# Counting table loads in the order, negating A's scores, four token tiles in the weights' room, and tile 5 of B's pairs 0 and 2 turned by VectorE and DMA

## The chip, the cores and the metric

The kernel runs on one core of one Trainium2 chip. The metric is the device time of one execution in microseconds (us). The core has five engines with a queue of instructions each: TensorE (PE in the profile), VectorE (DVE), ScalarE (ACT), GpSimd (POOL) and SyncE (SP), which here issues all DMAs.

## What is computed

One layer of a streaming encoder, for 1024 prompt tokens and 32 sample tokens with shared weights; the cache holds 512 earlier tokens for the sample. Everything is float32.

```python
u = rmsnorm(h, g_pre) @ w_in          # 1024 -> 4096: qA kA vA gA qB kB vB gB
# A: band attention, 8 heads x 64, chunks of 64, the own chunk and 8 before it
s = (qA @ kA.T) * SCALE + bias_table[:, clip(k_pos - q_pos, -128, 128) + 128]
oA = softmax(where(ok, s, -1e30)) @ vA
# B: stick-breaking attention, 8 heads x 64, strictly causal
z = (qB @ kB.T) * SCALE
log_1m = where(causal, log_sigmoid(-z), 0)
after = reversed_cumsum(log_1m) - log_1m
oB = where(causal, exp(log_sigmoid(z) + after), 0) @ vB
y = concat(oA * silu(gA), oB * silu(gB)) @ w_out
h = h + rmsnorm(y, g_post)
h = h + sigmoid(h @ w_ple_gate) * (p @ w_ple)
```

It returns the prompt's and the sample's h and the new keys and values of A and B.

## The kernel before

**Precision and layout.** Float32 products are made from two halves: a high part rounded to the type F32R (names with h) and the rest (names with l). The normalised input lies transposed in `hnh`/`hnl`, in three chunks of 352 tokens. A projection such as `kA1` (keys of A's pair 1) takes 24 matmuls of 352 columns per chunk into one of two `mm` banks (`col_steps`, L712), and ScalarE copies each bank into `stkA1`, `stqA1` or `stvA1`.

**Stages.** Heads go in pairs. The order of stages is A's pair 0, B's pair 0, A1, B1, A2, B2, A3, B3 (`pairs`, L1187). While the attention of one pair runs, the projections of the next pair are woven in (`weave`, L1255); behind the last pair come the gates, `w_ple`, the output product and the gate product of the last step.

**Attention of one head** (`attention`, L778). Its 1024 queries are eight tiles of 128. For tile i, `scores` (L813) makes the scores against the key blocks that it may see: all i+1 blocks in B, at most five in A. Scores of up to 512 columns lie in one of three banks `S` (names SA.., SB..), longer ones in two.
- In A, VectorE adds the bias and takes the row maximum in one instruction, a tiny TENSOR_SCALAR of one column negates it into `statA`, ScalarE makes Exp(score - maximum) with the row's sum, VectorE the reciprocal, GpSimd the product.
- In B, ScalarE makes Sigmoid(-z) into `om` and Sigmoid(z) into `be`, VectorE scans `om` backwards, and GpSimd multiplies. `om` and `be` are two arenas (`ring0`, 3,076 columns, and `ring1`, 3,640) from which each tile takes room in turn; room is free again when the tile that had it is done with.

**Turning the weights** (`weights_t`, L860). The value product needs the weights transposed, as `wTh` and `wTl`. There are two ways. The usual one is on TensorE: one transpose per block of 128 x 128, four to a bank `T` (names ptwA, ptwB), then ScalarE copies the bank to `wTh` and VectorE subtracts to get `wTl`. Tiles named in `ROUND` (L31) go round instead: VectorE transposes squares of 32 x 32 from `be` to `om` (STREAM_TRANSPOSE), one DMA writes that to DRAM (`swapB`), four DMAs read it back into `be` with the squares in place, and ScalarE's copy and VectorE's subtraction take it from there. Before, that was tile 5 in A and tiles 4 and 6 in B. `values` (L910) then makes the value product (PVA, PVB) for tiles 0 to 3 and for tiles 4 to 7.

**The order.** Nothing is issued where it is written. `Recorder` (L264) records every operation, with what it depends on and a class; `order` (L372) plays the whole program through with estimated durations (`cost`) and, whenever an engine is free, takes from what is ready the operation of the lowest class and earliest place. The result is the fixed order of each engine's queue; `emit` (L440) issues it, so all work has one line, L450, in the profile. After the change that line is L464. The estimates knew nothing of the instruction ACT_TABLE_LOAD, which stands in ScalarE's program wherever an Exp follows a Sigmoid or the reverse.

**Loading x.** `load_x` (L565) brings the nine token tiles in. Tiles 3 and 4 lie in the room that `wTh` will have later (`x34`, 33 x 128 columns); the others are in the `om` arena, which holds three tiles of 1,024 columns, so that tile 5 follows tile 0.

Of the kernel before, what the change touches and what calls it, by code (L numbers as in the profile page):

```python
# [13 lines left out]
P = 128  # L14
# [13 lines left out]

ROUND = {"A": ((5,),), "B": ((4,),(6,))}  # L31
LAG_T = 2
LAG_V = 2
SPACE_S = 0.1
# [138 lines left out]


class Op:
    __slots__ = ("eng", "what", "args", "kw", "key", "busy", "late", "ready", "left", "after", "at", "size", "shared")


LAND = {"PE": 165, "ACT": 0, "DVE": 0, "POOL": 0, "SP": 0, "CTL": 0}
SEM = 60  # L180
MARGIN = 400
ISSUE = 550
DMA_NS, DMA_RATE, DMA_MARGIN = 1500, 320.0, 2000
DVE_SET, POOL_SET = 137, 110

# [78 lines left out]
class Recorder:  # L264


    def __init__(self):
        self.ops, self.cls, self.low, self.closed, self.turns = [], 0, 0, [], []
        self.tensor = Engine(self, "PE", "tensor")
        self.vector = Engine(self, "DVE", "vector")  # L270
        self.scalar = Engine(self, "ACT", "scalar")
        self.gpsimd = Engine(self, "POOL", "gpsimd")
        self.sync = Engine(self, "SP", "sync")
# [26 lines left out]
    def node(self, eng, what, args, kw, after):  # L300
        o = Op()
        o.eng, o.what, o.args, o.kw, o.after = eng, what, args, kw, after
        o.key = (self.cls if eng == "PE" else self.low, len(self.ops))
        o.shared = False
        self.ops.append(o)
        return o

    def add(self, eng, what, args, kw):
        writes, reads = [], []
        method = what[1] if isinstance(what, tuple) else ""  # L310
        for i, a in enumerate(args):
            if isinstance(a, (View, Raw, Segments)):
                (writes if i == 0 or (method == "tensor_tensor_reduce" and i == 7) else reads).append(a)
        for k, a in kw.items():
            if isinstance(a, (View, Raw, Segments)):
                (writes if k in ("out", "accum_out") else reads).append(a)
        o = self.node(eng, what, args, kw, set())
        for mine, write in ((reads, False), (writes, True)):
            for v in mine:
                b = v.buf  # L320
                hit = False
                for other, box, wrote in b.uses:
                    if other is not o and (write or wrote) and all(p < y and x < q for (p, q), (x, y) in zip(v.box, box)):
                        o.after.add(other)
                        hit = True
                if b.pool is not None:
                    if not hit:
                        o.after.add(b.place)
                    b.pool.ops.append(o)
                b.uses.append((o, v.box, write))  # L330
        o.busy, o.late = self.cost(eng, method, args, kw, writes, reads)
        o.shared = eng == "POOL"
        if eng == "DVE":
            sbuf = [v for v in reads if isinstance(v, (View, Segments)) and not v.buf.psum and v.free() > 4]
            o.shared = len(sbuf) > 1 or (method == "tensor_copy" and len(sbuf) == 1 and not writes[0].buf.psum)
# [36 lines left out]
    def order(self):  # L372

        import heapq
        for place, old in self.turns:
            place.after.update(x[0] for x in old.uses)
        users = {id(o): [] for o in self.ops}
        for o in self.ops:
            o.left, o.ready = len(o.after), 0.0
            for a in o.after:  # L380
                users[id(a)].append(o)
        names = ("PE", "ACT", "DVE", "POOL", "SP", "CTL")
        free = dict.fromkeys(names, 0.0)
        soon = {e: [] for e in names}
        now = {e: [] for e in names}
        for o in self.ops:
            if not o.left:
                heapq.heappush(soon[o.eng], (0.0, o.key, id(o), o))
        out, port, line = [], 0.0, 0.0
        while len(out) < len(self.ops):  # L390
            best = None
            for e in names:
                if now[e]:
                    t = free[e]
                elif soon[e]:
                    t = max(free[e], soon[e][0][0])
                else:
                    continue
                if best is None or t < best[0]:
                    best = (t, e)  # L400
            t, e = best
            while soon[e] and soon[e][0][0] <= t:
                _, key, n, o = heapq.heappop(soon[e])
                heapq.heappush(now[e], (key, n, o))
            o = heapq.heappop(now[e])[2]
            if o.shared and e == "DVE" and port > t + DVE_SET:
                held = [x for x in now[e] if not x[2].shared]
                if held:
                    heapq.heappush(now[e], (o.key, id(o), o))
                    pick = min(held)  # L410
                    now[e].remove(pick)
                    heapq.heapify(now[e])
                    o = pick[2]
            o.at = t
            if e == "CTL":
                done = t
            elif e == "SP":
                free[e] = t + o.busy
                line = max(line, t + o.busy + DMA_NS) + o.late
                done = line + DMA_MARGIN  # L420
            else:
                if o.shared:
                    t = max(t, port - (DVE_SET if e == "DVE" else POOL_SET))
                    port = t + o.busy
                free[e] = t + o.busy
                done = t + o.busy + o.late
            out.append(o)
            for u in users[id(o)]:
                if u.eng == e and e != "SP":
                    r = t if e == "CTL" else free[e]  # L430
                else:
                    r = done + (0 if u.eng == "CTL" else SEM + (MARGIN if u.eng == "PE" else 0))
                u.ready = max(u.ready, r)
                u.left -= 1
                if not u.left:
                    heapq.heappush(soon[u.eng], (u.ready, u.key, id(u), u))
        return out
# [18 lines left out]
def stream_step(  # L456
# [108 lines left out]
    def load_x(t):  # L565
        n = min(P, T - t * P)
        if t == 3:
            x34.append(at.tile([P, ringh.cols], F32, tag="wTh", name="x34"))
        xt = x34[0][:, (t - 3) * D:(t - 2) * D] if 3 <= t < 5 else ring0.tile([P, D], f"x{t}")
        dma(xt[0:n], x_prompt[0, t * P:t * P + n, :] if t < 8 else x_sample[0])  # L570
        return xt, n

# [33 lines left out]
    def bias_rows():  # L606

        rb = ring0.tile([8, 257], "rb")
        dma(rb, rel_bias[0])
        R = ring1.tile([8, 768], "R")  # L610
        nc.gpsimd.memset(R, 0.0)
        nc.vector.tensor_scalar(R[:, 256:768], R[:, 256:768], rb[:, 0:1], None, ALU.add)
        nc.vector.tensor_copy(R[:, 0:256], rb[:, 0:256][:, ::-1])
        dma(r_dr, R)

# [96 lines left out]
    def col_steps(j):  # L712
# [7 lines left out]
        def mms(c, part):  # L720
# [24 lines left out]
                nc.gpsimd.tensor_tensor(sg, sg, box["og"], ALU.mult)  # L745
                dma(og_dr[n, :, cs], sg)
            elif k == "q":
                nc.scalar.activation(box["st"][:, cs], acc, AF.Copy, scale=SCALE)
            else:
                nc.scalar.copy(box["st"][:, cs], acc)  # L750

# [26 lines left out]
    def attention(ab, p, h):  # L778
# [5 lines left out]
        def begin():  # L784
            if ab == "A":
                bias = at2.tile([P, 640], F32, tag="bias", name=f"bias{nm}", bufs=2)
                dma(bias, bias_src(2 * p + h, P, 0, 640))
                nc.gpsimd.memset(bias[0:HD, 0:HD], NEG)
                nc.gpsimd.memset(bias[HD:P, 576:640], NEG)
                box["bias"] = bias  # L790

        def lo_block(i):
            return max(0, i - 4) if ab == "A" else 0

        together = {i: g for g in ROUND[ab] for i in g}
        whole, done_with = {}, []

        def cost(i):
# [14 lines left out]
        def scores(i):  # L813
# [27 lines left out]
            else:  # L841
                m = small.tile([P, 4], F32, tag="stat", name=f"stat{nm}_{i}", bufs=6)
                for j, (a, b, s) in enumerate(pieces):
                    nc.vector.tensor_tensor_reduce(
                        w0[:, a:b], s, box["bias"][:, n - b:n - a][:, ::-1], 1.0,
                        -3e38 if j == 0 else m[:, j - 1:j], ALU.add, ALU.max, m[:, j:j + 1])
                last = len(pieces) - 1
                nc.vector.tensor_scalar(m[:, 2:3], m[:, last:last + 1], -1.0, None, ALU.mult)
                nc.scalar.activation(w1[:, 0:n], w0[:, 0:n], AF.Exp, bias=m[:, 2:3], accum_out=m[:, 3:4])
                nc.vector.reciprocal(m[:, 3:4], m[:, 3:4])  # L850
                nc.gpsimd.tensor_scalar(w1[:, 0:n], w1[:, 0:n], m[:, 3:4], 1.0, ALU.mult, ALU.mult)
            state[i] = w0, w1
# [96 lines left out]
    def sample_attention(ab, gi):  # L949
# [45 lines left out]
        def scores():  # L995
# [20 lines left out]
            else:  # L1016
                m = small.tile([P, 4], F32, tag="stat", name="stat" + nm, bufs=6)
                for j, (a0, b0, s) in enumerate(pieces):
                    nc.vector.tensor_tensor_reduce(
                        w0[:, a0:b0], s, bx["bias"][:, NK - b0:NK - a0][:, ::-1], 1.0,  # L1020
                        -3e38 if j == 0 else m[:, 0:1], ALU.add, ALU.max, m[:, j:j + 1])
                nc.vector.tensor_scalar(m[:, 2:3], m[:, 1:2], -1.0, None, ALU.mult)
                nc.scalar.activation(w1[:, 0:NK], w0[:, 0:NK], AF.Exp, bias=m[:, 2:3], accum_out=m[:, 3:4])
                nc.vector.reciprocal(m[:, 3:4], m[:, 3:4])
                nc.gpsimd.tensor_scalar(w1[:, 0:NK], w1[:, 0:NK], m[:, 3:4], 1.0, ALU.mult, ALU.mult)
            bx["w1"] = w1
# [829 lines left out]
```

## Time and profile before

| what | us |
|---|---|
| median of 3 runs | 794.32 |
| lowest and highest run | 794.28, 794.92 |
| the profiled execution, whole | 794.5 |
| its span, first to last instruction | 792.7 |

The profile is of one execution. Its span leaves out 1.8 us around it. By stage (busy us of each engine; the stretches are cut near the first score matmul of each pair, the last near the output product; the start, and the stretch from 570 to 617 with the gates, are left out):

| stage | us | PE | DVE | ACT | POOL | DMA share |
|---|---|---|---|---|---|---|
| A0 | 60-109 | 48.22 | 37.08 | 36.23 | 35.41 | 0.88 |
| B0 | 109-173 | 62.70 | 52.90 | 47.67 | 43.12 | 0.64 |
| A1 | 173-229 | 56.00 | 43.32 | 40.87 | 39.39 | 0.77 |
| B1 | 229-308 | 78.16 | 62.70 | 57.58 | 58.51 | 0.71 |
| A2 | 308-353 | 43.47 | 33.28 | 37.91 | 24.32 | 0.61 |
| B2 | 353-420 | 66.51 | 50.49 | 49.12 | 32.28 | 0.41 |
| A3 | 420-478 | 56.41 | 44.51 | 41.72 | 24.41 | 0.53 |
| B3 | 478-570 | 91.86 | 67.52 | 56.25 | 55.34 | 0.60 |
| output and gate products | 617-793 | 170.67 | 137.59 | 112.85 | 106.54 | 0.69 |

How to read it: an engine's busy time is the sum of its instructions' stretches; matmuls overlap, so a busy PE says that something was under way, and what one matmul costs is read from start to start. In a row of the timeline stand the start in us, the duration, the engine, the line, the operation, what it writes <- what it reads, and in square brackets how long the engine was idle before it and for whom it waited. SPq stands for SyncE's queue, where the duration is that of issuing. Buffer numbers are left out of names, so that kA stands for every pair.

### The profile page before, as it was taken

The numbers are of one execution on the slowest core, as the hardware profiler recorded it, in microseconds if no ns is written. First come the engines' busy times: TensorE is split into PE (matmuls) and PEld (weight loads), VectorE is DVE, ScalarE is ACT, GpSimd is POOL, SyncE is SP. The second block draws the span as 40 slices with busy tenths as digits, with TensorE's granted clock in tenths as the row PEclk, the third lists the DMA queues.
The fourth block names the chain that finished last, engine by engine and source line by source line (L and its number), as shares of the span: only waits on it lengthen the run. The fifth ranks groups of instructions, "written<-read, shape, count | busy, mean of one in ns | idle before, by whom it ended". The sixth has DMA issues, their size and how long they took to land.

```text
span 792.7 us, 14512 instructions
## 1 busy us (share of the span) xinstructions
PE 778.6 (98%) x4606; PEld 717.9 (91%) x4606; DVE 587.4 (74%) x1170; ACT 537.3 (68%) x1173; POOL 470.1 (59%) x554
## 2 busy tenths in 40 slices
PE   8999999999999999999999999999999999999997
PEld 7999999899989998999998999999998787888786
DVE  7717778787778686877867788767565677988965
ACT  6636786786797677887766778664436976777551
POOL 5625867675777677454635246657462529599533
PEclk9999999999999999999999999999999999999999
DMA  8419866767866858544514746756589866859853
GB/s 296 138 49 289 215 188 213 189 189 226 229 192 205 232 176 238 144 128 123 142 54 132 172 111 175 225 167 188 151 261 291 282 190 186 288 168 336 272 170 133
DMA packets 161087, 153.66 MB, mean 194 GB/s; under 512 B 38562, under 2 KB 127178, under 8 KB 161011
## 3 DMA queue, kind: packets, MB, share of 16 engines
q1 hardware_dynamic: 161010, 152.73, 64.5%
q8 instruction: 37, 0.61, 0.3%
q14 instruction: 40, 0.32, 0.1%
HBM read 94.45 MB, written 49.83 MB: 182 GB/s over the span
## 4 chain that ended last, share of the span: by engine, by line
PE 84%; ACT 5%; DMA 3%; POOL 3%; DVE 3%; issue 2%; SPq 1%; DVEq 0%; ACTq 0%; POOLq 0%
PE mm_gA L450 6%; PE mm_gB L450 5%; PE mm_qB L450 5%; PE mm_vA L450 5%; PE mm_kB L450 5%; PE mm_qA L450 5%; PE PVB L450 4%; PE mm_kA L450 4%; PE SB L450 3%; PE mm_vB L450 3%; PE PVA L450 3%; PE SA L450 3%; PE g1P L450 2%; PE o3P L450 2%; PE o1P L450 2%; PE g0P L450 2%
## 5 line engine op out<-in xcount | busy, mean ns | idle before, releaser
L450 POOL TENSOR_TENSOR be<-be,om 128x1024 f32<-128x1024 f32 (+8 forms) x66 | 80.3, 1221 | 67.4 <-DVE om L450 34.0
L450 DVE TENSOR_TENSOR_SCAN om<-om,SB 128x384 f32<-128x384 f32 (+5 forms) x96 | 92.2, 966 | 14.5 <-ACT be L450 5.5
L450 POOL TENSOR_SCALAR be<-be,statA 128x640 f32<-128x640 f32 (+3 forms) x64 | 43.9, 691 | 52.8 <-DVE statA L450 37.0
L450 ACT ACTIVATE om<-SB 128x384 f32<-128x384 f32 (+5 forms) x96 | 46.6, 497 | 20.1 <-DVE SB L450 15.6
L450 ACT ACTIVATE be<-SB 128x384 f32<-128x384 f32 (+5 forms) x96 | 46.5, 498 | 13.4 <-DVE om L450 7.2
L450 ACT ACTIVATE be<-om,statA 128x640 f32<-128x640 f32 (+3 forms) x64 | 44.6, 697 | 15.5 <-DVE statA L450 11.3
L450 DVE TENSOR_TENSOR wTl<-ptwA,wTh 128x512 fp32r<-128x512 f32 (+2 forms) x80 | 36.2, 480 | 9.2 <-ACT wTh L450 8.9
L450 ACT CAST wTh<-ptwA 128x512 fp32r<-128x512 f32 (+2 forms) x80 | 32.1, 426 | 12.1 <-PE ptwA L450 10.4
L450 DVE TENSOR_TENSOR wTl<-ptwB,wTh 128x512 fp32r<-128x512 f32 (+3 forms) x64 | 33.7, 546 | 4.7 <-ACT wTh L450 4.3
L450 DVE CUSTOM_DVE_ANT_0 om<-SA,biasA 128x320 f32<-128x320 f32 (+2 forms) x64 | 30.9, 483 | 7.2 <-PE SA L450 5.6
L450 ACT CAST wTh<-ptwB 128x512 fp32r<-128x512 f32 (+3 forms) x64 | 29.6, 482 | 9.2 <-PE ptwB L450 5.9
L450 DVE TENSOR_TENSOR wTl<-be,wTh 128x640 fp32r<-128x640 f32 (+1 forms) x24 | 30.2, 1257 | 7.5 <-ACT wTh L450 7.4
L450 PE MATMUL SB<-kdB,LB 128*128 128x384 f32 (+5 forms) x96 | 33.4, 350 | 0.6 <-DVE om L450 0.6
L450 PE MATMUL SB<-klB,LB 128*128 128x384 f32 (+5 forms) x96 | 33.1, 347 | 0.0
L450 PE MATMUL ptwA<-ident,be 128*128 128x128 f32 x200 | 32.1, 273 | 0.5 <-DVE wTl L450 0.5
L450 PE MATMUL SA<-kdA,LA 128*128 128x320 f32 (+2 forms) x96 | 30.2, 323 | 1.7 <-DVE statA L450 0.9
L450 PE MATMUL ptwB<-ident,be 128*128 128x128 f32 x192 | 29.7, 274 | 0.6 <-POOL be L450 0.6
L450 PE MATMUL SA<-klA,LA 128*128 128x320 f32 (+2 forms) x96 | 29.1, 314 | 0.0
L450 POOL TENSOR_TENSOR oB<-oB,oB 128x256 f32<-128x256 f32 x32 | 25.5, 813 | 5.2 <-issue 3.5
L450 POOL TENSOR_TENSOR gB<-gB,gB 128x256 f32<-128x256 f32 x32 | 26.0, 837 | 2.4 <-DMA gB<-in_w_ple_gate_dram 1.8
L450 DVE TENSOR_TENSOR SB<-SB,maskb 128x128 f32<-128x128 f32 x64 | 17.6, 290 | 12.6 <-PE SB L450 10.0
L450 PEld LDWEIGHTS ptwA<-ident,be 128*128 128x128 f32 x200 | 24.2, 140 | 1.9 <-issue 1.0
(712 smaller groups left out, 2691.8 us busy)
## 6 DMA issues: line engine op xcount, KB each, us to landing
oB<-in_w_out_dram SPq DMA_DIRECT2D x16, 256.0 KB, 4.7
sum_dro<-oB SPq DMA_DIRECT2D x16, 256.0 KB, 2.4
gB<-in_w_ple_gate_dram SPq DMA_DIRECT2D x16, 256.0 KB, 3.8
sum_drg<-gB SPq DMA_DIRECT2D x16, 256.0 KB, 3.1
x<-in_x_prompt_dram SPq DMA_DIRECT2D x16, 256.0 KB, 4.6
h_dr<-h SPq DMA_DIRECT2D x8, 512.0 KB, 4.4
ht<-h_dr SPq DMA_DIRECT2D x8, 512.0 KB, 5.2
raw<-sum_drg SPq DMA_DIRECT2D x16, 256.0 KB, 3.5
```

Source lines behind the costliest of these rows:

```text
L450: getattr(getattr(tc.nc, o.what[0]), o.what[1])(*args, **kw)
```

## The change

It has four parts. (1) `ROUND` becomes `round_of`: in B's even pairs (0 and 2) tile 5 goes round too, and each round tile is a group of its own. (2) The order counts table loads: every Exp or Sigmoid depends on all operations of the table group before it, and `order` adds 1,280 ns to ScalarE's time where the table changes. (3) A's scores are made negative: q is copied with -SCALE, the bias is negated, the reduction takes the minimum, and Exp has scale -1 with that minimum as its bias, so the one-column negation goes. (4) Token tiles 3 to 6 instead of 3 and 4 lie in the room of `wTh`.

```diff
-ROUND = {"A": ((5,),), "B": ((4,),(6,))}
+def round_of(ab, p):
+    return (5,) if ab == "A" else (4, 5, 6) if p % 2 == 0 else (4, 6)
...
+TABLE = 1280
...
+        self.with_table, self.old_table = [], []
...
+        if method == "activation" and args[2] in (AF.Exp, AF.Sigmoid):
+
+            o.table = args[2]
+            if self.with_table and self.with_table[-1].table != o.table:
+                self.old_table, self.with_table = self.with_table, []
+            self.with_table.append(o)
+            o.after.update(self.old_table)
...
-        out, port, line = [], 0.0, 0.0
+        out, port, line, table = [], 0.0, 0.0, AF.Exp
...
+                if e == "ACT" and o.table not in (None, table):
+                    t, table = t + TABLE, o.table
...
-        xt = x34[0][:, (t - 3) * D:(t - 2) * D] if 3 <= t < 5 else ring0.tile([P, D], f"x{t}")
+        xt = x34[0][:, (t - 3) * D:(t - 2) * D] if 3 <= t < 7 else ring0.tile([P, D], f"x{t}")
...
+        nc.vector.tensor_scalar(rb, rb, -1.0, None, ALU.mult)
...
-                nc.scalar.activation(box["st"][:, cs], acc, AF.Copy, scale=SCALE)
+                nc.scalar.activation(box["st"][:, cs], acc, AF.Copy, scale=SCALE if ab == "B" else -SCALE)
...
-                nc.gpsimd.memset(bias[0:HD, 0:HD], NEG)
-                nc.gpsimd.memset(bias[HD:P, 576:640], NEG)
+                nc.gpsimd.memset(bias[0:HD, 0:HD], -NEG)
+                nc.gpsimd.memset(bias[HD:P, 576:640], -NEG)
...
-        together = {i: g for g in ROUND[ab] for i in g}
+        together = {i: (i,) for i in round_of(ab, p)}
...
-                        -3e38 if j == 0 else m[:, j - 1:j], ALU.add, ALU.max, m[:, j:j + 1])
+                        3e38 if j == 0 else m[:, j - 1:j], ALU.add, ALU.min, m[:, j:j + 1])
                 last = len(pieces) - 1
-                nc.vector.tensor_scalar(m[:, 2:3], m[:, last:last + 1], -1.0, None, ALU.mult)
-                nc.scalar.activation(w1[:, 0:n], w0[:, 0:n], AF.Exp, bias=m[:, 2:3], accum_out=m[:, 3:4])
+                nc.scalar.activation(w1[:, 0:n], w0[:, 0:n], AF.Exp, bias=m[:, last:last + 1], scale=-1.0, accum_out=m[:, 3:4])
```

The sample's attention gets the same edit of its A scores. Since the order is worked out anew, instructions move nearly everywhere. In all TensorE has 4,582 matmuls and transposes instead of 4,606, VectorE 140 TENSOR_SCALARs instead of 205, 53 STREAM_TRANSPOSEs instead of 49 and 616 TENSOR_TENSORs instead of 620, ScalarE 8 table loads instead of 12, and SyncE 760 DMAs instead of 740. Three places follow. In names, the digits behind A or B are pair, head and tile, and the last number of a name is that of the buffer.

The first place is ScalarE's queue at the change from B's pair 1 (scores SB11, head 1, tile 7) to A's pair 2 (statA20, head 0, tiles 0 to 2). Before:

```order
L450 COPY stkB2_4132<-mm_kB2_1_4115 128x352
L450 ACT_TABLE_LOAD
L450 ACTIVATE be_178,statA20_0_2909<-om_164,statA20_0_2909 128x128
L450 ACT_TABLE_LOAD
L450 ACTIVATE be_178<-SB11_7_0_3976 128x512
L450 ACTIVATE be_178<-SB11_7_1_4034 128x512
L450 ACT_TABLE_LOAD
L450 ACTIVATE be_178,statA20_1_2959<-om_164,statA20_1_2959 128x256
L450 ACTIVATE be_178,statA20_2_3073<-om_164,statA20_2_3073 128x384
```

After:

```order
L464 COPY stkB2_4090<-mm_kB2_0_3992 128x352
L464 ACTIVATE be_182<-SB11_7_0_3946 128x512
L464 ACTIVATE be_182<-SB11_7_1_4011 128x512
L464 ACT_TABLE_LOAD
L464 ACTIVATE be_182,statA20_0_2860<-om_168,statA20_0_2860 128x128
L464 ACTIVATE be_182,statA20_1_2932<-om_168,statA20_1_2932 128x256
L464 ACTIVATE be_182,statA20_2_3017<-om_168,statA20_2_3017 128x384
L464 COPY stkB2_4090<-mm_kB2_1_4077 128x352
```

Before, an Exp of A stands ahead of B's last two Sigmoids, with a load on each side of it and one more behind; after, the Sigmoids come first and one load stands between them and the Exps.

The second place is TensorE's queue in B's pair 0, from the first score tile of head 1 (SB01_0) to its second (SB01_1); ptwB00_5_4 are the last two transposes of head 0's tile 5, and mm_kA1 and mm_qA1 are projections of A's pair 1. Before:

```order
L450 MATMUL SB01_0_0_1801<-kdB01_1306,LB01_1311 128x128
L450 MATMUL SB01_0_0_1801<-klB01_1310,LB01_1311 128x128
L450 MATMUL mm_kA1_1_1716<-hnh1_140,wh_kA1_1_1425 128x352 x2
L450 MATMUL mm_kA1_1_1716<-hnh1_140,wl_kA1_0_1349 128x352 x4
L450 MATMUL mm_kA1_1_1716<-hnh1_140,wl_kA1_1_1366 128x352
L450 MATMUL ptwB00_5_4_1821<-ident_145,be_178 128x128 x2
L450 MATMUL mm_kA1_1_1716<-hnh1_140,wl_kA1_1_1366 128x352 x3
L450 MATMUL mm_kA1_1_1716<-hnl1_143,wh_kA1_0_1415 128x352 x4
L450 MATMUL mm_kA1_1_1716<-hnl1_143,wh_kA1_1_1425 128x352 x4
L450 MATMUL mm_kA1_2_1795<-hnh2_141,wh_kA1_0_1415 128x352 x3
L450 MATMUL SB01_1_0_1849<-kdB01_1306,LB01_1311 128x256
L450 MATMUL SB01_1_0_1849<-klB01_1310,LB01_1311 128x256
```

After:

```order
L464 MATMUL SB01_0_0_1811<-kdB01_1289,LB01_1293 128x128
L464 MATMUL SB01_0_0_1811<-klB01_1292,LB01_1293 128x128
L464 MATMUL mm_kA1_1_1705<-hnl1_147,wh_kA1_1_1373 128x352 x2
L464 MATMUL mm_kA1_2_1784<-hnh2_145,wh_kA1_0_1362 128x352 x4
L464 MATMUL mm_kA1_2_1784<-hnh2_145,wh_kA1_1_1373 128x352 x4
L464 MATMUL mm_kA1_2_1784<-hnh2_145,wl_kA1_0_1338 128x352 x4
L464 MATMUL mm_kA1_2_1784<-hnh2_145,wl_kA1_1_1348 128x352 x4
L464 MATMUL mm_kA1_2_1784<-hnl2_148,wh_kA1_0_1362 128x352 x4
L464 MATMUL mm_kA1_2_1784<-hnl2_148,wh_kA1_1_1373 128x352 x4
L464 MATMUL mm_qA1_0_1844<-hnh0_143,wh_qA1_0_1689 128x352 x4
L464 MATMUL SB01_1_0_1874<-kdB01_1289,LB01_1293 128x256
L464 MATMUL SB01_1_0_1874<-klB01_1292,LB01_1293 128x256
```

The transposes of tile 5 are gone (the four of its blocks 0 to 3 stood a little earlier), and 30 projection matmuls stand between the two score tiles instead of 21.

The third place is VectorE's queue in the same head, behind its value product of tiles 0 to 3 (PVB00_0) up to the subtractions of tiles 4 to 7 for `wTl`. Before:

```order
L450 TENSOR_TENSOR wTl_155<-be_178,wTh_499 128x4x5x32
L450 TENSOR_TENSOR otB00_0_0_1612<-PVB00_0_1672,otB00_0_0_1612 64x256
L450 TENSOR_TENSOR otB00_0_1_1724<-PVB00_0_1672,otB00_0_1_1724 64x256
L450 TENSOR_TENSOR wTl_155<-ptwB00_5_0_1788,wTh_499 128x512
L450 TENSOR_TENSOR wTl_155<-ptwB00_5_4_1821,wTh_499 128x256
L450 SCALAR_TENSOR_TENSOR om_164<-om_164,SB01_3_0_1871 128x512
L450 TENSOR_TENSOR SB01_4_1_2008<-SB01_4_1_2008,maskb_147 128x128
L450 TENSOR_TENSOR wTl_155<-be_178,wTh_499 128x4x7x32
L450 TENSOR_TENSOR wTl_155<-ptwB00_7_0_2009,wTh_499 128x512
```

After:

```order
L464 TENSOR_TENSOR wTl_159<-be_182,wTh_576 128x4x5x32
L464 TENSOR_TENSOR otB00_0_0_1604<-PVB00_0_1675,otB00_0_0_1604 64x256
L464 TENSOR_TENSOR otB00_0_1_1727<-PVB00_0_1675,otB00_0_1_1727 64x256
L464 TENSOR_TENSOR wTl_159<-ptwB00_7_0_1797,wTh_576 128x512
L464 SCALAR_TENSOR_TENSOR om_168<-om_168,SB01_1_0_1874 128x256
L464 SCALAR_TENSOR_TENSOR om_168<-om_168,SB01_2_0_1875 128x384
L464 SCALAR_TENSOR_TENSOR om_168<-om_168,SB01_3_0_1882 128x512
L464 TENSOR_TENSOR wTl_159<-be_182,wTh_576 128x4x6x32
L464 TENSOR_TENSOR SB01_4_1_2021<-SB01_4_1_2021,maskb_151 128x128
L464 TENSOR_TENSOR wTl_159<-be_182,wTh_576 128x4x7x32
```

The two subtractions of tile 5 from the banks ptwB00_5 are gone; one from `be` with 4x6x32 columns stands instead, two rows ahead of tile 6's (4x7x32), and three scans of head 1 ahead of it.

More of the change, by code (lines that the diff above doesn't have):

```diff
@@ L175 @@
 class Op:
-    __slots__ = ("eng", "what", "args", "kw", "key", "busy", "late", "ready", "left", "after", "at", "size", "shared")
+    __slots__ = ("eng", "what", "args", "kw", "key", "busy", "late", "ready", "left", "after", "at", "size", "shared", "table")
 LAND = {"PE": 165, "ACT": 0, "DVE": 0, "POOL": 0, "SP": 0, "CTL": 0}
@@ L303, in node @@
         o.key = (self.cls if eng == "PE" else self.low, len(self.ops))
-        o.shared = False
+        o.shared, o.table = False, None
         self.ops.append(o)
@@ L1020, in scores @@
                         w0[:, a0:b0], s, bx["bias"][:, NK - b0:NK - a0][:, ::-1], 1.0,
-                        -3e38 if j == 0 else m[:, 0:1], ALU.add, ALU.max, m[:, j:j + 1])
-                nc.vector.tensor_scalar(m[:, 2:3], m[:, 1:2], -1.0, None, ALU.mult)
-                nc.scalar.activation(w1[:, 0:NK], w0[:, 0:NK], AF.Exp, bias=m[:, 2:3], accum_out=m[:, 3:4])
+                        3e38 if j == 0 else m[:, 0:1], ALU.add, ALU.min, m[:, j:j + 1])
+                nc.scalar.activation(w1[:, 0:NK], w0[:, 0:NK], AF.Exp, bias=m[:, 1:2], scale=-1.0, accum_out=m[:, 3:4])
                 nc.vector.reciprocal(m[:, 3:4], m[:, 3:4])
```

## Prediction

> **What bounds the kernel now.** I read the page first: busy shares, the slices, the granted clock.
>
> ```profile
> span 792.7 us, 14512 instructions
> PE 778.6 (98%) x4606; PEld 717.9 (91%) x4606; DVE 587.4 (74%) x1170; ACT 537.3 (68%) x1173; POOL 470.1 (59%) x554
> PEclk9999999999999999999999999999999999999999
> ```
>
> TensorE (PE) is busy in 98% of the span, at the full clock in every slice, and no other engine passes 74%. Since a busy PE counts overlapping matmuls, the second view is what PE waited for (engine and tile waiting, releaser, us in total, times, longest).
>
> ```profile
> PE mm_kB L450 <- ACT stvA L450: 1.6, 1, 1.6
> ...
> PE PVB L450 <- DVE wTl L450: 1.3, 1, 1.3
> PE SA L450 <- DVE statA L450: 0.9, 2, 0.7
> PE SA L450 <- DVE LA L450: 0.8, 1, 0.8
> PE SB L450 <- DVE om L450: 0.6, 1, 0.6
> ```
>
> The largest wait is 1.6 us, and these five are 5.2 us. Only two things move the end: instructions leaving or joining PE's queue, and these waits growing or going. Work elsewhere counts only where PE then waits.
>
> **Tile 5 off TensorE.** In B's pairs 0 and 2, two heads each, tile 5 has six key blocks: 4 x 6 = 24 transposes leave PE's queue. Rows of one matmul last longer than its turn, so I price a transpose from start times. This is head 0 of pair 0; the x4 and the x2 are its tile 5.
>
> ```profile
> 129.76 0.60 PE L450 MATMUL ptwB<-ident,be 128*128 128x128 f32 x4
> 130.11 0.41 PE L450 MATMUL mm_kA<-hnh,wh_kA 128*128 128x352 f32 x1
> 130.35 0.22 PE L450 MATMUL SB<-kdB,LB 128*128 128x128 f32 x1
> ...
> 130.90 0.97 PE L450 MATMUL mm_kA<-hnh,wl_kA 128*128 128x352 f32 x5
> 131.71 0.38 PE L450 MATMUL ptwB<-ident,be 128*128 128x128 f32 x2
> 131.84 0.73 PE L450 MATMUL mm_kA<-hnh,wl_kA 128*128 128x352 f32 x3
> ```
>
> The five mm_kA from 130.90 to 131.71 take 0.162 us each. The x4 takes 0.35 us (129.76 to 130.11), and the mm_kA behind it 0.24 instead of 0.16: 0.43 in all, 0.11 each. The x2 takes 0.13 to the next start; with the same 0.08 on the mm_kA behind it that is 0.21, again 0.11 each. So 24 x 0.11 = **2.6 us** leave PE. Nothing joins it.
>
> What comes instead is on other engines. I take durations of the nearest shapes (640 and 896 columns; tile 5 has 768).
>
> ```profile
> L450 DVE STREAM_TRANSPOSE om<-be 128x640 f32<-128x640 f32 x16 | 13.4, 838 | 3.6 <-POOL be L450 2.9 <-POOL om L450 0.6
> L450 DVE STREAM_TRANSPOSE om<-be 128x896 f32<-128x896 f32 x8 | 8.8, 1103 | 0.3 <-POOL be L450 0.2
> L450 DVE TENSOR_TENSOR wTl<-be,wTh 128x640 fp32r<-128x640 f32 x16 | 17.4, 1085 | 5.0 <-ACT wTh L450 4.9
> L450 DVE TENSOR_TENSOR wTl<-be,wTh 128x896 fp32r<-128x896 f32 x8 | 12.8, 1600 | 2.5 <-ACT wTh L450 2.5
> L450 DVE TENSOR_TENSOR wTl<-ptwB,wTh 128x512 fp32r<-128x512 f32 x32 | 21.3, 679 | 2.6 <-ACT wTh L450 2.4
> L450 DVE TENSOR_TENSOR wTl<-ptwB,wTh 128x256 fp32r<-128x256 f32 x16 | 6.6, 409 | 0.5 <-ACT wTh L450 0.5
> L450 DVE TENSOR_SCALAR statA<-statA 128x1 f32<-128x1 f32 x64 | 9.5, 149 | 1.2
> L450 ACT ACT_TABLE_LOAD x12 | 15.4, 1283 | 0.9 <-PEq L1844 0.7
> ```
>
> Per head VectorE (DVE) gains a transpose (0.97, between 0.84 and 1.10) and a subtraction (1.34, between 1.09 and 1.60) and loses two from PSUM (0.68 + 0.41): +1.2 us, 4.9 over four heads. ScalarE swaps two copies for one, about even. Both have idle time beside PE, so I cost this at nothing; if the cover fails, the price is a wait of PE on wTl. What can fail is the trip's timing. Here is tile 6 of the same head, which goes round already.
>
> ```profile
> 133.75 1.10 DVE L450 STREAM_TRANSPOSE om<-be 128x896 f32<-128x896 f32 x1
> 134.88 0.34 SPq L450 DMA_DIRECT2D swapB<-om  x1
> 139.08 2.04 SPq L450 DMA_DIRECT2D be<-swapB  x3
> 146.73 0.94 ACT L450 CAST wTh<-be 128x896 fp32r<-128x896 f32 x1
> 148.09 4.09 DVE L450 TENSOR_TENSOR wTl<-be,wTh 128x896 fp32r<-128x896 f32 x1
> 149.80 1.43 POOL L450 TENSOR_TENSOR oB<-oB,oB 128x256 f32<-128x256 f32 x2
> 152.84 1.21 PE L450 MATMUL PVB<-wTl,v2B 128*128 128x512 f32 x4 [1.30 <-DVE wTl L450]
> ```
>
> From the VectorE transpose to the end of the subtraction it takes 18.4 us, and PE then waits 1.30 us for the value product PVB. Tile 5's trip adds five DMAs to SyncE's queue per head: 0.34 for the write and about 0.68 for each of four reads, 3 us, which tile 6's reads may now stand behind. The values of tiles 4 to 7 (PVB, second half) need both. Tile 5's rooms in the arenas also stay taken for its trip, and the next head's scores need them: in the new order 30 mm_kA matmuls (4.9 us by the row above) stand between SB01_0 and SB01_1, where 21 (3.4 us) stood before. So PE has other work there, taken from later in the stage; if the room comes later still, PE waits, which rival (2) prices with the rest. A new trip's wait was not seen; its bounds are nothing (seven of the eight heads with a tile 6 show no such wait as their longest) and 1.30 us per head. I take the frequency of the rows: one wait of 1.3 us in eight heads, 0.16 per trip, **+0.65 us** for four; zero and 5.2 are kept as ends.
>
> The 4.09 us there, against a mean of 1.60, ends just after GpSimd's row at 149.80 does (151.23). [...]
>
> [...]
>
> **Table loads.** ScalarE's program goes from 12 loads to 8, because every Exp of a pair now precedes the next pair's first Sigmoid and the reverse. By the row above that is 4 x 1.283 = 5.1 us of ScalarE. ScalarE does not bound; what counts is what stood behind. At the change from B's pair 1 to A's pair 2:
>
> ```profile
> 310.02 1.28 ACT L450 ACT_TABLE_LOAD   x1
> ...
> 311.32 1.09 ACT L450 ACTIVATE be<-SB 128x512 f32<-128x512 f32 x2
> ...
> 312.00 0.50 PE L450 MATMUL SA<-kdA,LA 128*128 128x512 f32 x1 [0.66 <-DVE statA L450]
> ...
> 314.35 0.17 DVE L450 RECIPROCAL statA<-statA 128x1 f32<-128x1 f32 x1 [2.41 <-ACT be L450]
> ...
> 314.54 1.09 PE L450 MATMUL ptwB<-ident,be 128*128 128x128 f32 x8 [0.58 <-POOL be L450]
> ```
>
> Behind A's first Exp come a load, two Sigmoids, another load and only then the next Exp (the order above shows them): VectorE waits with its reciprocal for 2.41 us with PE's next score banks behind it, and GpSimd gets its Sigmoids late. PE loses 0.66 and 0.58 us. The wait SB <- om (0.6) lies at the other place with two extra loads, the change from A's pair 1 to B's. I count **-1.9 us** (0.66 + 0.58 + 0.6). What comes instead: all first Sigmoids stand behind the last Exp, three score banks full, PE on projections meanwhile. Its bounds are nothing and the 1.28 us of a load; at three changes of pair I take **+0.3 us** together, near nothing, since PE has projection work queued there. The wait of 1.6 us (mm_kB <- ACT stvA) stays in the sum: the copy it waits for still stands right behind a load and an Exp.
>
> **Negated scores.** 64 TENSOR_SCALARs of 0.149 us and two like them leave VectorE, 9.8 us, against one over 8 rows of the bias table. They sat between each score tile's maximum and its Exp, 0.15 us on a chain that PE rarely waits for: 0.9 us in two waits over the whole run, partly counted above. I add nothing; bounds 0 and -0.2. The sign rides on the copy of q and on the Exp's scale.
>
> **Four token tiles.** Tiles 5 and 6 are loaded without waiting for tiles 0 and 1, two DMAs earlier in SyncE's queue, ahead of the masks and wr_vA. None of the waits names a load of x. Nothing; 0.5 us either way, if the first weights come behind them.
>
> **Sum.** 794.5 (profiled execution: span 792.7 and 1.8 around it) - 2.6 - 1.9 + 0.65 + 0.3 = 790.9. The median of the runs, 794.32, is 0.2 below that execution, so **790.7 us**.
>
> **Rivals.** (1) *Waits only move*: 5.2 us of small waits, and the 0.58 above, stay as much in a re-sorted program, only somewhere else. Then the transposes alone count: 794.3 - 2.6 = 791.7. For it: only three of these six waits hang together with the loads. Against it: those three stand at the loads that the new order leaves out.
> (2) *The trip is paid*: tile 6's reads behind tile 5's, or its rooms late, and all four heads wait 1.0 us (near the 1.30 above): 790.7 - 0.65 + 4.0 = 794.1. For it: SyncE's 3 us per head and the 18.4 us trip. Against it: tile 5's scores are ready a tile earlier than tile 6's, and its product stands where it stood.
> (3) *Slower, VectorE shut out by GpSimd*: each new subtraction is held as at 148.09, 4.09 - 0.95 (a free 768 by the lower rows) = 3.1 us, VectorE's scans and score banks behind it. It decides from 790.7 - 0.65 + 4w = 795.9, w = 1.5 us of PE wait per head; at 2.0 it gives 798.1. For it: the row. Against it: once in 24 such rows did it cost PE more than a microsecond.
> (4) *More goes than I count*: 1.6 and 1.3 vanish too in the re-sorted order: 787.8.
>
> **How the numbers follow.** Forecast 0.50, (1) 0.18, (2) 0.17, (3) 0.08, (4) 0.07. The measurement tells about 0.2%, 1.6 us, so faster is below 792.7 and slower above 795.9. Forecast, (1) and (4) lie on the fast side (0.75; I take 0.74 for the forecast's own spread), (2) inside (0.18), (3) slower (0.08). The range runs from 787.5, just below (4), to 794.6, past (2); (3) stays out.
>
> **What would show it.** Right: 24 fewer PE instructions, 8 loads, no wait of PE on statA or be at the change to A's pair 2, PVB <- wTl not above 2 us in all. Wrong: PVB <- wTl in each head of pairs 0 and 2; SB or mm waiting on ScalarE at a change to B; new wTl<-be,wTh rows of 3 us and more; or PE waits of still 5.8 us elsewhere.

## The result, and the profile after

The changed kernel took 790.43 us (median of 8 runs, 788.17 to 792.59), the kernel before 794.66 us (8 runs, 794.16 to 795.02): a ratio of 0.9949, 95% interval 0.9933 to 0.9964. That is 4.2 us quicker, and the interval stays clear of 1. The profiled execution of the changed kernel is its slowest, 792.59 us.

The first lines of its page, to be held against those of before (span and instructions, then busy us, share and instructions of each engine):

```profile
span 790.8 us, 14426 instructions
PE 776.3 (98%) x4582; PEld 716.2 (91%) x4582; DVE 592.1 (75%) x1105; ACT 532.7 (67%) x1165; POOL 475.3 (60%) x554
```

PE is busy for the same share as before, with 24 instructions fewer. What PE waited for (engine and tile, releaser, us in total, times, longest):

```profile
PE mm_kB L464 <- ACT stvA L464: 1.7, 2, 1.1
PE ptwA L464 <- DVE wTl L464: 1.5, 1, 1.5
PE idle L464 <- DVE newh L464: 1.3, 1, 1.3
PE ptwA L464 <- ACT ktB L464: 1.1, 1, 1.1
PE ptx L464 <- DVE be L464: 0.9, 2, 0.7
PE SA L464 <- DVE LA L464: 0.8, 1, 0.8
PE ptwsB L464 <- DVE wTl L464: 0.7, 1, 0.7
```

SA <- statA and SB <- om have gone, and mm_kB <- stvA has stayed, both as forecast; PVB <- wTl has gone too. Other names stand there instead. To compare whole executions I add up, from start to start of TensorE's rows, what goes beyond the usual spacing of that pair of shapes, and keep apart what is over 0.15 us in one place (waits) and what is less. Before: 753.3 us of matmuls, 11.0 of waits, 21.8 of small excess. This profile: 750.9, 12.4 and 21.1. So in the profiled execution matmuls and small excess fell by 3.1 us together, 2.4 of it counted as matmuls, and 1.4 came back as waits. The waits hardly depend on what is taken as the usual spacing; where the line lies between matmuls and small excess does (with the median spacing of all profiles the matmuls fall by 3.1 and the small excess by nothing).

Now the ScalarE queue at the change from B's pair 1 to A's pair 2 (timeline, columns as before):

```profile
309.32 0.60 ACT L464 ACTIVATE be<-SB 128x512 f32<-128x512 f32 x1 [2.60 <-DVE wTl L464]
309.93 1.28 ACT L464 ACT_TABLE_LOAD   x1
...
311.23 0.40 ACT L464 ACTIVATE be<-om,statA 128x128 f32<-128x128 f32 x1
...
312.96 1.04 PE L464 MATMUL ptwB<-ident,be 128*128 128x128 f32 x8
```

One load stands between the last Sigmoid and the first Exp, and the row of eight ptwB has no wait in brackets now. And the trip of tile 5 (768 columns) and tile 6 (896) in B's pair 0, head 0:

```profile
130.58 0.98 DVE L464 STREAM_TRANSPOSE om<-be 128x768 f32<-128x768 f32 x1
136.26 1.10 DVE L464 STREAM_TRANSPOSE om<-be 128x896 f32<-128x896 f32 x1
152.04 1.18 DVE L464 TENSOR_TENSOR wTl<-be,wTh 128x768 fp32r<-128x768 f32 x1
153.35 1.42 DVE L464 TENSOR_TENSOR wTl<-be,wTh 128x896 fp32r<-128x896 f32 x1
...
155.57 0.86 PE L464 MATMUL PVB<-wTl,v2B 128*128 128x512 f32 x3
```

Tile 5 is 22.6 us under way (130.58 to 153.22), longer than the 18.4 of tile 6 before, but the value product needs it only at 155.57 and has no wait.

The changed kernel's runs spread over 4.4 us, those of before over 0.9. A second profile of it (run `again` below, 788.83 us) has the same instructions in the same order, so its rows can be held against this one's, instruction by instruction. PE falls behind at two places, by 1.2 and 1.7 us, and at two more by 0.3 each. ScalarE's rows ahead of the two larger ones, first of this profile, then of `again`:

```profile
95.12 0.73 ACT L464 CAST wTh<-be 128x640 fp32r<-128x640 f32 x1 [3.92 <-DMA be<-swapA]
115.50 0.73 ACT L464 CAST wTh<-be 128x640 fp32r<-128x640 f32 x1 [2.10 <-DMA be<-swapA]
```

```profile
93.31 0.73 ACT L464 CAST wTh<-be 128x640 fp32r<-128x640 f32 x1 [1.98 <-DMA be<-swapA]
112.99 0.73 ACT L464 CAST wTh<-be 128x640 fp32r<-128x640 f32 x1 [0.73 <-POOL oB L464]
```

These are the trips of tile 5 in A's pair 0, which the change does not touch: the copies wait longer for their reads in this execution, 3.92 and 2.10 us. The DMA share of that stage doesn't tell why: it is 0.90 here and 0.92 in `again` (60 to 109 us). PE's rows that follow, from this profile:

```profile
97.68 0.63 PE L464 MATMUL ptwA<-ident,be 128*128 128x128 f32 x4 [1.06 <-ACT ktB L464]
118.54 0.63 PE L464 MATMUL ptwA<-ident,be 128*128 128x128 f32 x4 [1.54 <-DVE wTl L464]
```

### The profile page after: what moved, and what is told of

Read it like the earlier page. It is cut to its first block, busy times and chain, and to the rows that moved or that the text cites. A ratio compares the mean times of both kernels' runs of the same rounds, so it can differ in the third digit from the quotient of the medians.

```text
span 790.8 us, 14426 instructions
## 1 busy us (share of the span) xinstructions
PE 776.3 (98%) x4582; PEld 716.2 (91%) x4582; DVE 592.1 (75%) x1105; ACT 532.7 (67%) x1165; POOL 475.3 (60%) x554
## 4 chain that ended last, share of the span: by engine, by line
PE 84%; POOL 4%; DMA 3%; DVE 3%; ACT 2%; issue 1%; SPq 1%; ACTq 0%; DVEq 0%; POOLq 0%
PE mm_gB L464 6%; PE mm_gA L464 6%; PE mm_qA L464 5%; PE mm_kB L464 5%; PE mm_kA L464 5%; PE mm_vA L464 5%; PE mm_vB L464 4%; PE PVB L464 4%; PE mm_qB L464 4%; PE SB L464 4%; PE PVA L464 3%; PE SA L464 3%; PE g1P L464 2%; PE o3P L464 2%; PE o1P L464 2%; PE g0P L464 2%
## 5 line engine op out<-in xcount | busy, mean ns | idle before, releaser
L464 POOL TENSOR_TENSOR be<-be,om 128x256 f32<-128x256 f32 (+8 forms) x66 | 87.7, 1335 | 58.3 <-DVE om L464 37.5
L464 DVE TENSOR_TENSOR wTl<-be,wTh 128x640 fp32r<-128x640 f32 (+2 forms) x28 | 36.3, 1298 | 6.5 <-ACT wTh L464 5.9
L464 DVE TENSOR_TENSOR wTl<-ptwB,wTh 128x512 fp32r<-128x512 f32 (+3 forms) x56 | 29.5, 546 | 7.7 <-ACT wTh L464 4.6
L464 ACT CAST wTh<-ptwB 128x512 fp32r<-128x512 f32 (+3 forms) x56 | 26.0, 484 | 11.3 <-PE ptwB L464 7.7
L464 DVE STREAM_TRANSPOSE om<-be 128x640 f32<-128x640 f32 (+2 forms) x28 | 26.1, 932 | 2.8 <-POOL be L464 2.4
L464 ACT CAST wTh<-be 128x640 fp32r<-128x640 f32 (+2 forms) x28 | 22.5, 805 | 7.0 <-DMA be<-swapA 6.4
```

The costliest lines, as they stand in the source:

```text
L464: getattr(getattr(tc.nc, o.what[0]), o.what[1])(*args, **kw)
```

## The experiments

Twelve runs; each ratio is against the kernel before, run on the same chip. "Waits" is the sum of PE's excess over 0.15 us in the run's one profile, worked out as above. The profiled execution isn't always the median one: that of tables_only took 791.92 us, for instance, that of neg_back 791.38 and that of resort_after 793.49.

| run | us, median (lowest to highest) | ratio, 95% interval | loads | waits |
|---|---|---|---|---|
| again | 789.35 (788.83 to 789.81) | 0.9935, 0.9923 to 0.9947 | 8 | 8.9 |
| loads_inplace | 795.55 (794.21 to 798.44) | 1.0014, 1.0004 to 1.0023 | 8 | 11.9 |
| double_turns | 813.55 (813.50 to 814.21) | 1.0243, 1.0230 to 1.0256 | 12 | 10.1 |
| trip_only | 797.73 (796.07 to 799.15) | 1.0039, 1.0028 to 1.0051 | 10 | 16.1 |
| tables_only | 793.77 (791.85 to 796.12) | 0.9987, 0.9977 to 0.9998 | 8 | 8.9 |
| no_trip | 789.17 (788.01 to 789.46) | 0.9924, 0.9912 to 0.9936 | 8 | 7.2 |
| signs_only | 799.95 (798.03 to 803.80) | 1.0067, 1.0046 to 1.0089 | 16 | 14.9 |
| resort | 800.92 (799.96 to 802.34) | 1.0079, 1.0067 to 1.0091 | 12 | 16.1 |
| no_tables | 797.25 (797.03 to 798.36) | 1.0037, 1.0024 to 1.0049 | 12 | 15.0 |
| resort_after | 792.40 (791.60 to 793.88) | 0.9973, 0.9964 to 0.9981 | 8 | 10.7 |
| resort_no_trip | 789.41 (789.31 to 790.21) | 0.9938, 0.9925 to 0.9950 | 8 | 6.2 |
| neg_back | 790.01 (789.01 to 791.46) | 0.9941, 0.9927 to 0.9955 | 8 | 11.0 |

**again.** The changed kernel, not edited.

> The changed kernel once more, unaltered. Its eight runs lay between 788.17 and 792.59 us, while those of before lay within 0.9 us, and its profile is of the slowest of them. Theory of the prediction: median 790.4, ratio 0.995, and another profile shows 24 transposes fewer again; what differs between a quick and a slow execution are waits of PE, not matmuls. Rival: the spread came from one chip; then the runs lie within 1 us here.

All five runs lie within 1 us, at the quick end of the first eight. All thirteen executions have their median at 789.61; I use that below. Between the two that were profiled, most of the difference is the two waits shown above; of the others no profile exists.

**double_turns.** What does a transpose cost?

```diff
                 if isinstance(o.what, tuple):
-                    getattr(getattr(tc.nc, o.what[0]), o.what[1])(*args, **kw)
+                    for _ in range(2 if o.what[1] == "transpose" and o.args[0].buf.name.startswith("ptwB") else 1):
+                        getattr(getattr(tc.nc, o.what[0]), o.what[1])(*args, **kw)
```

> Before, with each of the 192 TensorE transposes of B's weights issued twice, the second over the first; every queue is else as before. Theory of the prediction: 0.11 us each, so 192 x 0.11 = 21 us more, 815.6 us. Rival: the rows' own mean of 0.274 us is the price, 52 us more, 847 us. Rival on the other side: part of a transpose hides behind the matmul after it, so a second one in a run costs half, 10 us more, 805 us.

18.9 us for 192 more, 0.0986 us each, so 24 are 2.4 us. The group's row shows why its mean is no price: 384 transposes keep a mean of 273 ns, 105 us if they stood one behind the other, but the group is busy for 50.5 us, because rows overlap.

```profile
L451 PE MATMUL ptwB<-ident,be 128*128 128x128 f32 x384 | 50.5, 273 | 0.6 <-POOL be L451 0.6
```

**loads_inplace.** Are the four loads worth 1.9 us by themselves? ScalarE's finished queue is rewritten when it is issued; all other queues stay.

```diff
     def emit(self, tc):
-        ops = self.order()
+        ops = self.merged(self.order())
...
+        for o in act:
+            g = group.get(id(o))
+            if g is not None and g > now:
+                held.append(o)
+                continue
+            line.append(o)
+            if g is not None:
+                left[g] -= 1
+                while now < len(left) - 1 and not left[now]:
+                    now += 1
+                    line += [x for x in held if group[id(x)] == now]
...
```

> Before, with one thing altered: ScalarE's queue keeps all Exps of a pair ahead of the next pair's first Sigmoid and the reverse (8 table loads instead of 12), by moving those rows alone; every other queue has the order of before. Theory of the prediction: PE's waits SA <- statA (0.66), ptwB <- be (0.58) and SB <- om (0.6) go, 1.9 us, so 792.7 us (ratio 0.9976), with at most 0.3 lost behind the loads that are left. Rival, waits only move: 794.3 or more, since the Sigmoids or Exps that are held back let PE wait at the same places for as long.

It is 0.9 us slower. Against before, instruction by instruction, PE is 0.3 us behind from the start on. It gains 1.4 us at and behind the change to A's pair 2, where two loads go: SA no longer waits for statA, at two places. The wait of ptwB for be, which the forecast let go too, stays as it was:

```profile
315.94 1.09 PE L503 MATMUL ptwB<-ident,be 128*128 128x128 f32 x8 [0.62 <-POOL be L503]
```

PE loses 2.0 us at the change from A's pair 1 to B's, where the other two loads go. There, ScalarE, VectorE and PE of this run:

```profile
229.26 0.82 ACT L503 ACTIVATE be<-om,statA 128x640 f32<-128x640 f32 x1
...
230.17 1.28 ACT L503 ACT_TABLE_LOAD   x1
231.47 0.28 ACT L503 ACTIVATE om<-SB 128x128 f32<-128x128 f32 x1
231.64 0.27 ACT L503 ACTIVATE be<-SB 128x128 f32<-128x128 f32 x1
```

```profile
232.01 0.42 DVE L503 TENSOR_TENSOR_SCAN om<-om,SB 128x128 f32<-128x128 f32 x1 [3.42 <-ACT be L503]
```

```profile
232.49 0.79 PE L503 MATMUL SB<-kdB,LB 128*128 128x512 f32 x1 [2.06 <-DVE statA L503]
```

B's first Sigmoids stand behind A's last Exps and the load. VectorE's scan waits 3.42 us for them, and PE waits 2.06 us with a score matmul next in its queue. (The row names statA, which VectorE finished at that moment; the scan that empties a score bank ended at 232.43, 0.06 us earlier.) Before, the Sigmoids of B's first two score tiles stood ahead of those Exps, at the price of two loads. So here a load saved was no gain, since the queues of the other engines expected its rows earlier.

**trip_only, signs_only, resort.** The first and third part of the change alone, and a control that removes nothing.

```diff
-MARGIN = 400
+MARGIN = 420
```

> Before with the first part of the change alone: tile 5 of B's pairs 0 and 2 goes round, and the order is worked out anew without counting table loads (it has 10 of them). Theory of the prediction: 2.6 us of transposes go and 0.65 us of waits come, 792.6 us. Rival, the trip is paid: PE waits about 1 us in each of four heads, 795.9 us. Rival, transposes alone: 791.9 us.

> Before with the third part alone (negated scores); the order is worked out anew without counting loads, and has 16 of them. Theory of the prediction: nothing to -0.2, 794.5 us. New theory: its order is another one, with four loads more that no one counted, so its PE waits are longer: 796 us or more.

> Before with one constant of the order's estimates altered (MARGIN, what is added where PE waits for another engine, from 400 to 420 ns): the same instructions in a slightly other order. Theory of the prediction: nothing, 794.6 us within 0.4, since no instruction leaves. New theory: any new order shifts the time by its own PE waits, 1 us or more either way.

All three are slower, by 3.1, 5.3 and 6.2 us. `resort` has the same instructions as before and 20 ns more in an estimate; so the order of before is a good one among those that don't count loads (five of them: 794.6, 797.3, 797.7, 800.0 and 800.9 us), and a comparison of one part with before mixes the part with a new order. The longest waits of trip_only (the two left out lie at the start):

```profile
PE SB L452 <- ACT be L452: 1.7, 1, 1.7
PE SB L452 <- DVE LB L452: 1.5, 1, 1.5
PE mm_vA L452 <- ACT wh_vA L452: 1.4, 2, 0.8
...
PE mm_qB L452 <- ACT stqB L452: 1.2, 1, 1.2
PE mm_kB L452 <- ACT stvA L452: 1.1, 1, 1.1
```

Four of these five wait for ScalarE, and none is PVB <- wTl; the last stands in before's list too, with 1.6 us.

**tables_only, no_tables.** The second part alone, and the change without it.

```diff
         if method == "activation" and args[2] in (AF.Exp, AF.Sigmoid):
 
-            o.table = args[2]
-            if self.with_table and self.with_table[-1].table != o.table:
-                self.old_table, self.with_table = self.with_table, []
-            self.with_table.append(o)
-            o.after.update(self.old_table)
+            pass
```

> Before with the second part alone: the order is worked out with 1,280 ns for a table load and with Exps and Sigmoids kept apart (8 loads); tile 5 is turned on TensorE as before. Theory of the prediction: -1.9 + 0.3, so 793.0 us. New theory, after loads_inplace: fewer loads alone are worth 1.4 us at one place and cost 2.3 at another, and what a new order brings is the sum of its own waits, which the trace lists: the time then follows PE's waits, and can lie 2 us on either side of 794.6.

> The changed kernel without its second part: trip, signs and token tiles stay, the order is worked out without counting loads (12 of them). Theory of the prediction: the loads' -1.9 + 0.3 come back, 791.6 us. New theory: an order that doesn't count the loads is late on ScalarE wherever it believed otherwise, as in resort (800.9), signs_only (800.0) and trip_only (797.7), so 796 to 801 us, with 12 us or more of PE waits.

tables_only is 0.9 us quicker than before, somewhat over half of the forecast 1.6, and 7.2 quicker than `resort`, which has the same matmuls in an order that doesn't count loads. Without the second part the change takes 797.25 us, 7.6 more than with it (789.61). The second part does two things, it keeps Exps and Sigmoids apart and it adds 1,280 ns, and no run has one without the other. In the profile of no_tables ScalarE stands between A's pair 0 and B's pair 0 like this:

```profile
104.68 1.28 ACT L460 ACT_TABLE_LOAD   x1
105.97 0.28 ACT L460 ACTIVATE om<-SB 128x128 f32<-128x128 f32 x1
...
106.64 1.28 ACT L460 ACT_TABLE_LOAD   x1
107.94 0.84 ACT L460 ACTIVATE be<-om,statA 128x640 f32<-128x640 f32 x1
...
109.35 1.28 ACT L460 ACT_TABLE_LOAD   x1
110.64 0.28 ACT L460 ACTIVATE be<-SB 128x128 f32<-128x128 f32 x1
```

Three loads in 6 us, two of them between the two Sigmoids of one score tile. PE loses 0.66, 0.72 and 0.93 us beyond the usual spacing at 107.75, 109.39 and 110.98 us, and that stage (first score matmul of B's pair 0 to that of A's pair 1) takes 69.5 us, against 66.9 in the changed kernel's profile and 65.3 in `again`.

**no_trip, resort_after, resort_no_trip.** Tile 5 back on TensorE, in the changed kernel and in another order of it (MARGIN 420 as above).

```diff
 def round_of(ab, p):
-    return (5,) if ab == "A" else (4, 5, 6) if p % 2 == 0 else (4, 6)
+    return (5,) if ab == "A" else (4, 6)
```

> The changed kernel with tile 5 of B's pairs 0 and 2 turned on TensorE again (24 transposes back), parts 2 to 4 kept. Theory of the prediction: 790.0 (the changed kernel's runs) + 2.4 (24 x 0.0986, from double_turns) - 0.65 = 791.8 us. Rival: the trip was what cost or brought more than its transposes, by the rooms and the queue: then it differs from that by over 1.5 us.

> The changed kernel with MARGIN at 420 instead of 400 ns, the alteration that cost the kernel before 6.2 us. New theory: where loads are counted, another order costs much less, so 788 to 793 us. Rival, the changed kernel's order is as lucky as that of before was: 795 us or more.

> As the run before it (MARGIN 420), with tile 5 of B's pairs 0 and 2 on TensorE: a second pair of orders with and without the trip. Theory of the prediction: 1.9 us slower than resort_after. Rival, as no_trip was: the trip gives back what its 24 transposes save, within 1 us of resort_after, or quicker than it.

Where loads are counted, the same 20 ns shift the time by 0.2 us without the trip and 2.8 with it, instead of 6.2. And the trip, with the order that it brings, is worth nothing in either pair: 789.61 with it against 789.17 without, 792.40 against 789.41. The 2.4 us of transposes are given back and more. PE's waits say so too: 8.9 (`again`) against 7.2, 10.7 against 6.2. But the waits that come are mostly not at tile 5's product: PVB waits 0.2 us in resort_after, at 152.06, where ScalarE's copy of tile 6 had waited 1.11 us for its reads. The longest of resort_after (one of 1.3 at the start is left out):

```profile
PE ptwsB L464 <- DVE wTl L464: 1.7, 2, 0.9
...
PE ple L464 <- ACT wph0True L464: 1.1, 1, 1.1
PE ptosB L464 <- DVE wTl L464: 1.1, 1, 1.1
```

These belong to the sample's attention (sB) in B's odd pairs and to the start. no_trip has the lowest median here, and resort_no_trip is 0.06 us behind `again`. All but two of their ten executions lie within the spread of the changed kernel's (788.17 to 792.59); I don't call them quicker than it.

**neg_back.** The changed kernel in its own order, with the work of the 64 negations put back.

```diff
+                if id(o) in self.small_after:
+                    src, dst = (x.get() for x in self.small_after[id(o)])
+                    tc.nc.vector.tensor_scalar(dst, src, 1.0, None, ALU.mult)
```

> The changed kernel in its own order, with one TENSOR_SCALAR of one column put back behind the last reduction of each of the 64 score tiles of A, and Exp reading its result. Theory of the prediction: 0 to 0.2 us more than the changed kernel's 789.4 to 790.4. Rival: 64 x 0.149 us on the chain from a score to its Exp is what shortened PE's waits, so 1.5 us more or above, 791.5.

790.01 us against 789.61. The five executions spread over 2.5 us (789.01 to 791.46), and the intervals of this run and of `again` overlap nearly whole, each about 2 us wide. So no worth of the negations is seen; one of about 1 us isn't excluded.

## Why the prediction was right, and where it was not

The time was forecast at 790.7 and came to 790.43, within the range and on the side forecast. The sum behind it holds less well: two terms were mis-sized, in opposite directions, and that they cancel is luck. (Summed without rounding, the three waits are 1.84 and the forecast 790.8. Of the 30 matmuls that it calls mm_kA, four are mm_qA.)

- **Tile 5 off TensorE, -2.6.** Shown right as a price: 0.0986 us each, 2.4 us for 24.
- **The trip, +0.65.** As far as two pairs of orders tell, this term was too small. The place I named is quiet: PVB has no wait for wTl in the changed kernel's lists. None of rival (3)'s 2.0 us waits of PE appeared. But with the trip the kernel takes the same time as without it, or 3.0 us more: that makes 2.8 us of cost in the one pair and 5.4 in the other (the 2.4 and the difference), each with the new order that the trip brings. Rival (2) had a price between these, at another place. How the trip makes waits far from its own product isn't shown. One candidate is the arena rooms that it holds longer, another that two orders simply differ by that much; two pairs don't tell them apart.
- **VectorE's new rows.** Their means are near the estimates (0.98 and 1.41, forecast 0.97 and 1.34), but the second mean hides what rival (3) named. Three of the four new subtractions of the changed kernel take 0.95 to 1.18 us; the one in pair 2, head 0, takes 2.55, in both profiles. A row of GpSimd (385.65, 2.60 us) that began 0.87 us earlier ends at 388.25, and the subtraction ends 0.82 us behind it, as the one of 4.09 us before ended 0.95 behind GpSimd's:

```profile
386.52 2.55 DVE L464 TENSOR_TENSOR wTl<-be,wTh 128x768 fp32r<-128x768 f32 x1
```

  PE did not wait there. In neg_back's profile another of the four takes 2.14 us, up to 182.38, and PE waits from there on, 0.73 us:

```profile
180.24 2.14 DVE L466 TENSOR_TENSOR wTl<-be,wTh 128x768 fp32r<-128x768 f32 x1
...
183.11 0.41 PE L466 MATMUL SA<-kdA,LA 128*128 128x320 f32 x1 [0.73 <-DVE statA L466]
```

  So a long subtraction with a wait of PE behind it does occur, at one place of one profile, and far from PVB. That GpSimd shuts VectorE out, as rival (3) has it, was my estimate; the rows show how long they last and when they end, not what holds them.
- **Table loads, -1.9 and +0.3.** The mechanism was half right. At the change to A's pair 2 SA's wait for statA went, and in place two loads less brought 1.4 us there, where I had counted 0.66 + 0.58; but the 0.58 (ptwB <- be) stayed in place, and went only with the new order. At the change to B's pair 1 I credited 0.6, and in place it cost 2.0, beyond the 1.28 that I had set as the bound of a wait behind a load. What pays is an order that is worked out with the loads counted and the two functions kept apart: 7.6 us between no_tables and the changed kernel. Only part of that shows against before, since before's order is 6.2 us better than its neighbour `resort`.
- **Negated scores, nothing.** Not contradicted (neg_back), but only to about 1 us.
- **Four token tiles, nothing.** Not run alone. The first score matmul of A's pair 0 starts at 64.8 us in the changed kernel and 64.5 before, so no gain is seen at the place where x is used.
- **Rival (1), waits only move.** In the profiled execution it nearly describes what happened (waits 11.0 before, 12.4 after), and my own sign of being wrong, PE waits of still 5.8 us elsewhere, is nearly met there: ptwA, mm_kB, ptwsB and mm_gA wait 5.6 us together. In `again` the waits are 8.9, and small excess 20.8 instead of 21.8: 2.4 + 2.1 + 1.0 make up its 5.5 us.

So parts two to four together bring 5.3 to 5.5 us (no_trip and resort_no_trip against before), where I had 1.6, and the trip brings none, where I had 2.0. Why tables_only stays 4.6 us behind no_trip, although no worth of the negations is seen in place, is open: x's room, or again one order against another.

## What to carry to other kernels

Where a scheduler sets the order, one edit measured against the order that happens to be there tells little: run a control that only re-sorts (here 20 ns in an estimate: 6.2 us), and test an edit in an unaltered order, by rewriting the finished queues. A known cost that the scheduler's model leaves out (here 1.28 us per table load) was worth more in the model, together with the rule that keeps the two functions apart, than out of the program: 7.6 us quicker against 0.9 slower. A transfer of work off the bounding engine is credited only after a run with and one without it, since its price can fall due far from the place that was edited.

## What the runs showed of the hardware

I had not expected that a wait of PE costs more than its length. In loads_inplace, behind the 2.06 us wait (columns: stretch, length, busy us of PE, PEld, DVE, ACT, POOL with counts, granted clock, DMA share, GB/s):

```profile
230.00:232.40 2.40, 0.43 (x4) 0.23 (x2) 0.39 (x2) 2.38 (x7) 0.00 (x0) 0.99 0.51 150
232.40:234.00 1.60, 1.51 (x4) 1.32 (x5) 1.23 (x7) 0.48 (x3) 1.48 (x3) 0.50 0.96 259
234.00:236.00 2.00, 2.00 (x10) 1.83 (x9) 1.97 (x3) 1.69 (x4) 2.00 (x6) 0.56 1.10 264
```

The granted clock is 0.50 from 232.4 to about 235.8 us, so that 3.4 us of matmuls do the work of 1.7 (their usual spacings add up to that; the four PVA<-wTh, for one, take 1.16 us to the next start, 234.69 to 235.85, and 0.66 in the profile of before). The same happened in resort_after (302.3 to 305.8), no_tables (110.8 to 114.2), trip_only (279.2 to 282.6) and signs_only (111.7 to 115.1), each time behind two or three waits close together, with as little as 1.53 us of idle in all (resort_after, 0.45 and 1.08):

```profile
300.00:302.00 2.00, 0.77 (x5) 0.56 (x5) 1.94 (x6) 1.93 (x4) 1.74 (x1) 1.00 0.45 113
302.00:304.00 2.00, 2.00 (x9) 2.00 (x9) 2.00 (x6) 1.98 (x4) 1.92 (x2) 0.58 1.01 308
304.00:306.00 2.00, 2.00 (x10) 2.00 (x8) 1.96 (x3) 1.33 (x2) 1.92 (x3) 0.56 0.97 256
```

Single waits of 1.72 us (resort_no_trip) and 1.63 us (resort) left the clock at 1.00, and so did two of 1.17 and 0.76 us that end 1.9 us apart (signs_only, at 233.27 and 235.20). So the idle time alone doesn't decide, and how much is enough isn't shown. What the five profiles share is the length: the clock stays at 0.50 for about 3.4 us in each, by windows of 0.5 us. In the profiles of before, of the changed kernel and of `again` the clock stays at 1.00 up to the last matmul, so this plays no part between those; of the 3.0 us by which resort_after is slower than resort_no_trip it can be about 1.5, an estimate from the usual spacings of the matmuls in that stretch (1.9 us of work in 3.5).
